# An input projection fed by unscaled x: 1/rms moved from the operand to the projected tiles

## The chip, the core and the metric

The kernel runs on one core of a Trainium2 chip. The metric is the device time of one execution in microseconds (us). The core's engines work side by side, each through its own queue: TensorE (PE in the profile, PEld for its weight loads), VectorE (DVE), ScalarE (ACT), GpSimd (POOL) and SyncE (SP, which here issues nearly all DMAs).

## What is computed

One layer of a streaming encoder, for 16 meta tokens, 64 tokens of running streams and 1024 prompt tokens at once (model width 2048):

```python
xn = _rmsnorm(h, norm_w)                       # x * rsqrt(mean(x^2) + eps) * norm_w
proj = jnp.einsum('bld,dp->blp', xn, w_in)     # 2048 -> 8208
a_b, a_c, a_x, a_z, qkv, z_b, b_logit, a_logit = jnp.split(proj, PROJ_CUTS, axis=-1)
y_a = a_b * _causal_conv(concat(state, a_c * a_x), conv_a_w) * silu(a_z)      # mixer A
qkv_c = silu(_causal_conv(concat(state, qkv), conv_qkv_w))                    # mixer B
o = gated_delta_net(l2norm(q), l2norm(k), v, beta, g)                         # in chunks
y_b = _rmsnorm(o, o_norm_w) * silu(z_b)
out = _rmsnorm(h + concat(y_a, y_b) @ w_out, final_norm_w)
```

The mean of squares is over the 2048 channels of a token; `norm_w` is one factor per channel. So the factor 1/rms of a token can be applied before the projection or after it, while `norm_w` has to be applied before it.

## The kernel before

x lies transposed (channels on the partitions) as 16 blocks of 128 channels, and its columns, the tokens, are cut into three pieces (`PIECES`): piece 0 has 336 columns (meta, streams, 256 of the prompt), pieces 1 and 2 have 384 each. Every fp32 operand is split into two exact parts, `xh`/`xl` and `wh`/`wl`, and a product is three matmuls (`xh*wh`, `xl*wh`, `xh*wl`). A *tile* of the projection is 128 output channels; per piece it takes 16 blocks x 3 = 48 matmuls into one PSUM bank of the pool `pj` (4 banks). The weights of a tile come as four chunks of 128x512 (256 KB), loaded on SP; ScalarE makes `wh` (128x512 CAST) and VectorE makes `wl` (128x512 TENSOR_TENSOR); `Weights.get` splits some chunks ahead (`ahead`), into as many places as there are buffers.

When the matmuls of a tile are done, `post` takes its pieces out of PSUM with the first stage of `a_tile`, `b_tile` or `z_tile`, and puts the rest (convolution, tanh, products) into `convs`, whose stages `pump` hands out beside the matmuls that follow, by the added-up costs `clk` of the engines; `flush_convs` hands out what is left at the end of a tile. Beside all this runs the delta net (`dn_front`, `dn_back`), whose blockwise inversion works on GpSimd (lines 787 to 796).

Before piece 0 enters the projection it is multiplied by `norm_w` alone, and its 1/rms (`rs0`) multiplies each tile as VectorE takes it out of PSUM. Pieces 1 and 2 are multiplied by 1/rms before the split: `x_later` (line 515) goes over every pair of blocks twice, first for the squares (ScalarE squares, GpSimd adds them up, line 480), then, once `x_rstd` (line 482) has the 1/rms on all partitions, to scale (GpSimd, line 534) and to split (`x_split`, line 507: ScalarE `xh`, VectorE `xl`). For piece 2 the second pass loads the pair again. The tiles of pieces 1 and 2 therefore leave PSUM without a factor: ScalarE copies them (lines 307, 338), or takes the tanh straight out of PSUM, or VectorE multiplies them by what is at hand.

`x_rstd` is a chain: 6 small matmuls sum the squares over the partitions (`ssx`), 13 VectorE instructions on 128x3 compute the inverse root, one makes diagonal matrices (`dg`), matmuls with ones spread them (`rsx`), ScalarE copies the result.

The prologue (lines 453 to 585) projects the first two channel blocks of mixer A in 24 single-piece tiles: all 8 for piece 0 (the first two side by side, chunk by chunk, with `W.ahead = 1`), then all 8 for piece 1, then all 8 for piece 2. After it come beta and decay (line 590 on) and the 56 remaining tiles, each with all three pieces, then the output projection.

VectorE executes in the order in which the code issues its instructions (the kernel is built with `manual_schedule(engines={DVE})`, line 1191). For the other engines the compiler's scheduler orders instructions by when it believes them ready; an engine then runs that order strictly.

Of the kernel before, what the change touches and what calls it, by code (L numbers as in the profile page):

```python
# [28 lines left out]
# columns of x^T: 16 meta tokens, 64 of the sample stream, 1024 of the prompt  # L29
# [5 lines left out]
# columns of the constants  # L35
# [5 lines left out]
# columns of the packed small parameters  # L41
# [4 lines left out]
class Timed:  # L46
    """An engine whose work is added up, so that the order of the program can follow it."""
# [19 lines left out]
def hymba_kernel(ctx: ExitStack, tc: tile.TileContext, hT, x_prompt, x_sample, w_in, w_ba, w_out, cst1, cst2, par,  # L67
# [27 lines left out]
    # three 128x128 blocks, their rows 416 apart and the blocks 4448, so that the twelve 32x32 blocks on the diagonals  # L95
    # are an equal step of 4448 apart too
# [30 lines left out]
    rs0 = const([P, PIECES[0][1]], "rs0")  # L127
# [8 lines left out]
    t32 = [const([P, 3, P], f"t32_{i}") for i in range(2)]  # L136
# [28 lines left out]
    # ---------------------------------------------------------------- work that goes on beside the projections  # L165
# [106 lines left out]
    def z_tile(h, p, ps):  # L272
        t = cvt("th")
        if p == 0:
            zr = cvt("zr")
            V.tensor_tensor(zr[:, :320], ps[:, 16:336], rs0[:, 16:336], ALU.mult)
            S.activation(t[:, :320], zr[:, :320], AF.Tanh, scale=0.5)
            yield
# [12 lines left out]
    def b_tile(h, w, p, ps):  # L291
        """conv, SiLU (twice its value) of a piece of q, k or v, or the gate; to the scratch memory."""
# [12 lines left out]
        else:  # L305
            n = PW
            S.copy(raw[:, 3:387], ps[:, :PW])
# [23 lines left out]
    def a_tile(j, w, p, ps):  # L331
        """the parts of mixer A of a channel tile, in the order C, X, Z, B"""
        if w == AC:
# [3 lines left out]
            else:  # L337
                S.copy(cs, ps[:, :PW])
            apc[p] = cs
        elif w == AX:  # L340
            cs = apc[p]
            u = cvt("u")
            if p == 0:
                n = 322
                t = cvt("xt", "acc")
# [7 lines left out]
            else:  # L353
                n = PW
                V.tensor_tensor(u[:, 2:386], ps[:, :PW], cs, ALU.mult)
# [7 lines left out]
        elif w == AZ:  # L363
            acc = apc[p]
            zr = cvt("za")
            if p == 0:
                V.tensor_tensor(zr[:, 0:320], ps[:, 16:336], rs0[:, 16:336], ALU.mult)
                yield
                t = cvt("th", "acc")
                S.activation(t[:, 0:320], zr[:, 0:320], AF.Tanh, scale=0.5)  # L370
                V.scalar_tensor_tensor(zr[:, 0:320], t[:, 0:320], 1.0, zr[:, 0:320], ALU.add, ALU.mult)
                V.tensor_tensor(acc[:, 0:64], zr[:, 0:64], acc[:, 0:64], ALU.mult)
                V.tensor_tensor(acc[:, 66:322], zr[:, 64:320], acc[:, 66:322], ALU.mult)
            else:
                S.activation(zr[:, :PW], ps[:, :PW], AF.Tanh, scale=0.5)
                V.scalar_tensor_tensor(zr[:, :PW], zr[:, :PW], 1.0, ps[:, :PW], ALU.add, ALU.mult)
                yield
                V.tensor_tensor(acc, zr[:, :PW], acc, ALU.mult)
        else:
            acc = apc.pop(p)  # L380
            y = cvt("ya", "raw")
            m = 320 if p == 0 else PW
            if p == 0:
                V.tensor_tensor(y[:, :m], ps[:, 16:336], rs0[:, 16:336], ALU.mult)
                yield
                V.tensor_tensor(y[:, :64], y[:, :64], acc[:, :64], ALU.mult)
# [8 lines left out]
    def post(kind, i, w, p, ps):  # L395
        """takes a piece out of PSUM at once; the rest of its work goes on beside what follows"""
# [10 lines left out]
    # ---------------------------------------------------------------- input projection  # L407
# [6 lines left out]
    jobs = [("a", j, w, (p,)) for p in ALLP for j in (0, 1) for w in AORD]  # L414
    NFIRST = len(jobs) // 3
# [10 lines left out]
    def project(js, first=lambda k: None):  # L426
        """tiles of the projection side by side: {(kind, head or block, part, piece): its place in PSUM}"""
        ps = {}
        for j in js:
            for p in j[3]:  # L430
                ps[j[:3] + (p,)] = pj.tile([P, 512], F32, tag="pj", name=f"pj{p}")
# [20 lines left out]
    # ---------------------------------------------------------------- prologue: x^T  # L452
    with ExitStack() as pro:
        xs = pro.enter_context(tc.tile_pool(name="xs", bufs=1))
        pp = pro.enter_context(tc.tile_pool(name="pp", bufs=1, space=PSUM))
        one = xs.tile([P, P], F32, tag="one", name="one")
        V.memset(one, 1.0)
        W = stream[0] = Weights(chunks[:12 * NFIRST], [P, 4, P], (wpool, "w", (2, 2)), (xs, "p", (2, 2)))

        def x_load(o, p, k, n):  # L460
            a, m = PIECES[p]
            Q.dma_start(o[:, :, :m], hT[:, k:k + n, a:a + m])

        def x_pair(p, i):
            n = PIECES[p][1]
            if p < 2:
                return raws[p][:, 2 * i:2 * i + 2, :n]
            t = xs.tile([P, 2, PW], F32, tag="xr", name="xr", bufs=3)
            x_load(t, p, 2 * i, 2)
            return t  # L470

        def x_square(t, acc, i, eng):
            n = t.shape[2]
            d = acc if i == 0 else xs.tile([P, 2, PW], F32, tag="sq", name="sq", bufs=2)
            if eng is S:
                S.activation(d[:, :, :n], t, AF.Square)
            else:
                eng.tensor_tensor(d[:, :, :n], t, t, ALU.mult)
            if i:
                G.tensor_tensor(acc[:, :, :n], acc[:, :, :n], d[:, :, :n], ALU.add)  # L480

        def x_rstd(p, acc, out):
            """(mean of the squares + eps)^-1/2 of every token, on all partitions"""
# [6 lines left out]
            yield X_LAG[2]  # L490
# [9 lines left out]
            yield X_LAG[3]  # L500
# [4 lines left out]
            S.copy(out[:, :n], ps[:, :n])  # L505

        def x_split(p, i, t):
            for j in range(2):
                k, n = 2 * i + j, t.shape[2]
                w = pk[:, K_NW + k:K_NW + k + 1]  # L510
                S.activation(xh[p][:, k, :n], t[:, j], AF.Copy, scale=w)
                V.scalar_tensor_tensor(xl[p][:, k, :n], t[:, j], w, xh[p][:, k, :n].bitcast(F32), ALU.mult,
                                       ALU.subtract)

        def x_later(p):
            acc = xs.tile([P, 2, PW], F32, tag="acc", name="sqa")
            ahead = deque()
            for i in range(NK):
                # every pair of tiles twice
                while len(ahead) < (3 if p == 2 else 1) and i + len(ahead) < NK:  # L520
                    ahead.append(x_pair(p, (i + len(ahead)) % 8))
                t = ahead.popleft()
                if i < 8:
                    x_square(t, acc, i, S)
                    yield X_LAG[0]
                    continue
                if i == 8:
                    yield X_LAG[1]
                    rsb = xs.tile([P, PW], F32, tag="rsb", name="rsb")
                    yield from x_rstd(p, acc, rsb)  # L530
                    yield X_LAG[4]
                    if p == 2:
                        x_tiles(2)
                G.tensor_tensor(t, t, rsb[:, None, :].to_broadcast([P, 2, PW]), ALU.mult)
                yield X_LAG[5]
                x_split(p, i - 8, t)
# [663 lines left out]
```

## Time and profile before

| | us |
|---|---|
| median of 3 runs | 2288.12 (2285.22 to 2289.0) |
| span of the profiled execution | 2283.8 |
| TensorE busy in it | 2211.3 (97%) |
| VectorE busy | 1335.5 (58%) |
| ScalarE busy | 640.1 (28%) |
| GpSimd busy | 940.4 (41%) |

The profiled execution has no time of its own beside its span; the span is 4.3 us under the median of the timed runs, which also hold what lies around the first and last instruction. TensorE's records overlap (one matmul begins before the one before it has left the array), so its pace is read from the distance of starts, or from counts in a window, not from the duration of one record. The granted clock is 1.00 at 2.4 GHz and 0.50 at 1.2 GHz.

### The profile page before, as it was taken

The page shows a single profiled execution, that of the slowest core. Times are in us where ns is not written, and L with a number is a line of the kernel's source. Part 1 is how long each engine was busy: PE and PEld are TensorE (multiplying, and loading weights), DVE is VectorE, ACT ScalarE, POOL GpSimd, SP SyncE. Part 2 cuts the span into 40 slices and gives each one's busy share as a digit, 9 for nine tenths or more (in the row PEclk, how much of TensorE's full clock was granted, in tenths as well). Part 3 has the DMA queues.
Part 4 walks back from the last instruction along what each step waited for, and adds up shares of the span by engine and source line. Part 5 has one row for each costly group of instructions (what it writes and reads, how often), then busy time and mean ns, then how long its engine had stood idle before and what let it go on. Part 6 is the DMA issues. An engine that isn't in the chain of part 4 may idle for free.

```text
span 2283.8 us, 36007 instructions
## 1 busy us (share of the span) xinstructions
PE 2211.3 (97%) x12938; PEld 2074.7 (91%) x12938; DVE 1335.5 (58%) x3421; ACT 640.1 (28%) x1575; POOL 940.4 (41%) x1557
## 2 busy tenths in 40 slices
PE   7799999999999999999999999999999999999998
PEld 6699889999999999999999999999999997788886
DVE  7964355667576547655664567456645345464544
ACT  5443122222222222222222222122222125444341
POOL 4520006657466645555665666655464300000000
PEclk9999999999999999999999999999999999999999
DMA  6444223232323222322222222222222238654652
GB/s 224 148 154 142 64 65 90 69 95 70 91 84 91 71 76 81 97 64 77 80 78 73 79 81 86 73 61 83 86 80 63 62 97 279 216 192 153 217 175 83
DMA packets 168790, 242.69 MB, mean 106 GB/s; under 512 B 18332, under 2 KB 92260, under 8 KB 168484
## 3 DMA queue, kind: packets, MB, share of 16 engines
q1 hardware_dynamic: 163076, 228.84, 32.1%
q0 software_dynamic: 3072, 7.11, 1.7%
q10 hardware_dynamic: 2464, 4.46, 0.5%
q8 instruction: 101, 1.65, 0.3%
q14 instruction: 77, 0.63, 0.1%
HBM read 196.14 MB, written 44.17 MB: 105 GB/s over the span
## 4 chain that ended last, share of the span: by engine, by line
PE 82%; DVE 11%; DMA 2%; issue 2%; ACT 2%; POOL 0%; SPq 0%; DVEq 0%; ACTq 0%; POOLq 0%
PE pj L83 58%; PE po L83 16%; DVE acc L61 2%; PE psy L83 2%; DVE wl L61 2%; DMA yr<-yscr 1%; PE psx L83 1%; PE psm L83 1%; PE psn L83 1%; PE pjb L83 1%; PE psu L83 1%; PE psr L83 1%; ACT jk L61 1%; DVE rot L61 1%; DVE xl L61 1%
## 5 line engine op out<-in xcount | busy, mean ns | idle before, releaser
L83 PE MATMUL pj<-xh,wh 128*128 128x384 f32 x2048 | 692.9, 338 | 8.0 <-DVE raw L61 3.5
L83 PE MATMUL pj<-xl,wh 128*128 128x384 f32 x2048 | 690.6, 337 | 1.1 <-DVE xl L61 1.1
L83 PE MATMUL pj<-xh,wl 128*128 128x384 f32 x2048 | 690.5, 337 | 0.5 <-DVE wl L61 0.4
L61 DVE TENSOR_TENSOR wl<-wr,wh 128x512 fp32r<-128x512 f32 x496 | 371.2, 753 | 343.3 <-ACT wh L61 341.7
L83 PE MATMUL pj<-x,wh 128*128 128x320 f32 (+3 forms) x2048 | 530.6, 340 | 9.4 <-ACT x L61 6.5
L61 ACT CAST wh<-wr 128x512 fp32r<-128x512 f32 x496 | 305.3, 618 | 719.1 <-PE pj L83 522.8
L792 POOL TENSOR_TENSOR tm<-eT 12x30 f32<-12x30 f32 (+4 forms) x720 | 392.1, 545 | 127.3 <-DMA eT<-e_in 72.8
L794 POOL TENSOR_TENSOR eT<-eT,tm 12x30 f32<-12x30 f32 (+4 forms) x720 | 418.5, 581 | 56.4
L83 PEld LDWEIGHTS pj<-xh,wh 128*128 128x128 f32 x2048 | 385.4, 188 | 12.7 <-issue 4.0
L83 PEld LDWEIGHTS pj<-xl,wh 128*128 128x128 f32 x2048 | 385.1, 188 | 2.1 <-DVE xl L61 1.7
L83 PEld LDWEIGHTS pj<-xh,wl 128*128 128x128 f32 x2048 | 384.9, 188 | 1.4 <-DVE wl L61 1.4
L83 PEld LDWEIGHTS pj<-x,wh 128*128 128x128 f32 x2048 | 353.7, 193 | 21.1 <-ACT x L61 6.5
L83 PE MATMUL pj<-x,wl 128*128 128x320 f32 (+3 forms) x1024 | 324.0, 316 | 11.0 <-DVE wl L61 10.9
L83 PE MATMUL po<-wh,yh 128*128 128x512 f32 x656 | 238.9, 396 | 2.6 <-DVE yh L61 1.9
L787 POOL DMA_DIRECT2D eT<-e_in x24 | 17.1, 711 | 504.6 <-DMA e_in<-bm 318.9
L83 PE MATMUL po<-wl,yh 128*128 128x512 f32 x528 | 208.9, 396 | 1.9 <-DVE wl L61 1.9
L83 PEld LDWEIGHTS pj<-x,wl 128*128 128x128 f32 x1024 | 196.9, 192 | 13.7 <-DVE wl L61 13.7
L1058 POOL TENSOR_TENSOR hres<-hres,fw 128x512 f32<-128x512 f32 x1 | 1.7, 1732 | 481.4 <-ACT hres L61 481.4
L83 PEld LDWEIGHTS po<-wh,yh 128*128 128x128 f32 x656 | 123.2, 188 | 34.0 <-ACT wh L61 3.1
L61 DVE SCALAR_TENSOR_TENSOR acc<-raw,pk,acc 128x384 f32<-128x384 f32 (+1 forms) x216 | 147.5, 683 | 5.8
L83 PE MATMUL po<-wh,yl 128*128 128x512 f32 x336 | 132.8, 395 | 0.0
L83 PEld LDWEIGHTS po<-wl,yh 128*128 128x128 f32 x528 | 99.1, 188 | 27.7 <-DVE wl L61 4.1
(254 smaller groups left out, 2191.3 us busy)
## 6 DMA issues: line engine op xcount, KB each, us to landing
wr<-in_w_in SPq DMA_DIRECT2D x320, 256.0 KB, 3.1
wr<-in_w_out SPq DMA_DIRECT2D x176, 256.0 KB, 2.7
scr<-acc SPq DMA_DIRECT2D x48, 192.0 KB, 1.9
kq<-scr SPq DMA_DIRECT2D x48, 192.0 KB, 3.0
hres<-in_x_prompt SPq DMA_DIRECT2D x32, 256.0 KB, 5.3
xr<-in_hT SPq DMA_DIRECT2D x16, 384.0 KB, 4.2
yr<-yscr SPq DMA_DIRECT2D x32, 192.0 KB, 3.4
scr<-co SPq DMA_DIRECT2D x24, 192.0 KB, 1.9
```

The lines of the kernel that those rows point to most:

```text
L61: return fn(out, *a, **k)
L83: T.matmul(out, lhsT, rhs, start=start, stop=stop)
L787: G.dma_start(eT, blocks(e_in[i]))
L792: G.tensor_tensor(t, eT[:, j + 1:32, j:j + 1].to_broadcast([12, n, j]), eT[:, j:j + 1, 0:j].to_broadcast([12, n, j]), ALU.mult)
L794: G.tensor_tensor(eT[:, j + 1:32, 0:j], eT[:, j + 1:32, 0:j], t, ALU.add)
L1058: G.tensor_tensor(o, o, fw[:r, ns], ALU.mult)
```

## The change

1. All three pieces are split unscaled (times `norm_w` only) and read once. The first pass of `x_later` is gone, as are GpSimd's additions (line 480) and multiplications (line 534). ScalarE still squares (in place, after the split); VectorE adds the squares (`x_sum`, 7 additions of two blocks per piece). Piece 2 is loaded once.
2. `rs` holds 1/rms of all three pieces, and each tile of pieces 1 and 2 is multiplied by it on VectorE as it leaves PSUM: in place of ScalarE's copy for q, k, v and C, as one more instruction for X, Z, B and the gate of mixer B. Tanh then reads SBUF.
3. The first two channel blocks go in another order and shape: block 0 for piece 0 (4 tiles, the first two side by side), block 1 for pieces 0 and 1 together (4), block 0 for pieces 1 and 2 (4), block 1 for piece 2 (4): 16 tiles and 64 chunks of weights in place of 24 and 96. They are held in PSUM (`held`, a second pool `pf` of 3 banks beside `pj`) until the 1/rms of their piece is there; `settle` then posts them in order. The splits of piece 1 are issued chunk by chunk within tile 5 (`second`), those of piece 2 within tile 9 (`third`), the sums within tiles 4, 6 and 9.
4. In `dn_back`, `tt` and `t64` share the places of `ti` and `b32`; `t32` moves to another pool. (For room in SBUF.)

The core of the diff:

```diff
     def b_tile(h, w, p, ps):
...
-            S.copy(raw[:, 3:387], ps[:, :PW])
+            V.tensor_tensor(raw[:, 3:387], ps[:, :PW], rs[p], ALU.mult)
     def a_tile(j, w, p, ps):
...
-                S.copy(cs, ps[:, :PW])
+                V.tensor_tensor(cs, ps[:, :PW], rs[p], ALU.mult)
...
-                V.tensor_tensor(u[:, 2:386], ps[:, :PW], cs, ALU.mult)
+                V.tensor_tensor(t, ps[:, :PW], rs[p], ALU.mult)
+                V.tensor_tensor(u[:, 2:386], t, cs, ALU.mult)
...
-    jobs = [("a", j, w, (p,)) for p in ALLP for j in (0, 1) for w in AORD]
-    NFIRST = len(jobs) // 3
+    jobs = [("a", j, w, ps) for j, ps in ((0, (0,)), (1, (0, 1)), (0, (1, 2)), (1, (2,))) for w in AORD]
+    NFIRST = len(jobs)
...
-                G.tensor_tensor(acc[:, :, :n], acc[:, :, :n], d[:, :, :n], ALU.add)
...
-                G.tensor_tensor(t, t, rsb[:, None, :].to_broadcast([P, 2, PW]), ALU.mult)
...
+        def x_squares(p, kc):
+            for k in range(kc, kc + 4, 2):
+                o = raws[p][:, k:k + 2, :PIECES[p][1]]
+                S.activation(o, o, AF.Square)
+
+        def x_sum(p, kc):
+            t = raws[p]
+            for o, m in (((0, 8), (2, 8)), ((4, 8), (6, 8)), ((0, 4), (2, 4)), ((0, 2),))[kc // 4]:
+                a, b = (t[:, k:k + 2, :PIECES[p][1]] for k in (o, o + m))
+                V.tensor_tensor(a, a, b, ALU.add)
...
+        def second(kc):
+            if kc not in split[1]:
+                split[1].add(kc)
+                for k in range(kc, kc + 4):
+                    x_split(1, k, raws[1][:, k, :PIECES[1][1]])
+                x_squares(1, kc)
+            settle()
+
+        def third(kc):
+            if kc not in split[2]:
+                split[2].add(kc)
+                for _ in range(2):
+                    x2_pair()
+            settle()
...
+        def settle(every=False):
+            while held:
+                _, key, ps = held[0]
+                if ("rs", key[3]) not in done:
+                    if not every:
+                        break
...
+                held.popleft()
+                if key[:3] != last[0]:
+                    flush_convs()
+                last[0] = key[:3]
+                post(*key, ps)
...
+        hooks = {2: and_settle(squares_and_load), 3: and_settle(x_sum, 0), 4: second, 5: and_settle(x_sum, 1), 8: third}
+        for i in range(2, NFIRST):
...
+            hold(1, hooks.get(i, lambda kc: settle()), pool)
+            if i in (3, 5):
+                p = i // 5
+                running[f"rs{p}"] = [0.0, known(p, x_rstd(p, raws[p]))]
```

## Rows read from the trace of the kernel before

**Rows 1.** The page: busy tenths of PE in 40 slices of 57 us.
```profile
PE   7799999999999999999999999999999999999998
```

**Rows 2.** Windows: busy us (xrecords) of PE, PEld, DVE, ACT, POOL; clock; DMA share; GB/s.
```profile
80.00:100.00 20.00, 12.62 (x64) 12.12 (x65) 19.89 (x19) 5.60 (x11) 17.15 (x9) 0.76 0.37 111
...
600.00:1000.00 400.00, 395.77 (x2511) 384.69 (x2510) 240.93 (x685) 96.12 (x278) 248.04 (x438) 1.00 0.27 80
```

**Rows 3.** Windows within the prologue, same columns.
```profile
6.50:25.00 18.50, 15.44 (x48) 12.66 (x49) 18.10 (x16) 13.16 (x25) 14.31 (x9) 1.00 0.67 233
...
43.50:50.00 6.50, 0.12 (x1) 0.01 (x1) 6.26 (x9) 2.19 (x3) 5.53 (x4) 0.66 0.18 64
...
51.20:55.70 4.50, 4.50 (x19) 4.50 (x18) 3.63 (x11) 2.54 (x4) 1.46 (x1) 0.50 0.84 260
```

**Rows 4.** Waits of PE, whole span: us in total, times, longest.
```profile
PE rsx L83 <- DVE dg L61: 13.5, 2, 7.1
PE pj L83 <- DVE wl L61: 11.3, 10, 3.3
...
PE pj L83 <- DVE raw L61: 3.5, 2, 1.9
```

**Rows 5.** Timeline of PE in the prologue: start, us, what, count, [idle before].
```profile
6.54 0.64 PE L83 MATMUL pj<-x,wh 128*128 128x322 f32 x1 [6.54 <-ACT x L61]
```
```profile
8.88 0.47 PE L83 MATMUL pj<-x,wl 128*128 128x322 f32 x1
```
```profile
32.45 0.46 PE L83 MATMUL pj<-x,wh 128*128 128x320 f32 x2
...
35.09 0.46 PE L83 MATMUL pj<-x,wh 128*128 128x320 f32 x2
```
```profile
50.02 1.54 PE L83 MATMUL rsx<-dg,one 128*128 128x128 f32 x6 [6.39 <-DVE dg L61]
```
```profile
106.62 0.33 PE L83 MATMUL pj<-xh,wh 128*128 128x384 f32 x1
```

**Rows 6.** Timeline of DVE in the prologue.
```profile
41.83 1.79 DVE L61 SCALAR_TENSOR_TENSOR rxy<-rxt,rxy 128x3 f32<-128x3 f32 x1
```
```profile
87.81 2.02 DVE L61 SCALAR_TENSOR_TENSOR cs<-u,cah,cs 128x322 f32<-128x322 f32 x1
...
102.69 0.48 DVE L61 TENSOR_TENSOR za<-pj,rs 128x320 f32<-128x320 f32 x1
...
110.83 5.38 DVE L61 SCALAR_TENSOR_TENSOR xl<-raw,pk,xh 128x384 fp32r<-128x384 f32 x10
```
```profile
128.31 0.22 DVE L61 TENSOR_SCALAR v<-ssx 128x2 f32<-128x2 f32 x2
...
129.36 0.16 DVE L61 SCALAR_TENSOR_TENSOR rxy<-rxt,rxy 128x3 f32<-128x3 f32 x1
...
131.21 0.42 DVE L61 TENSOR_SCALAR cs<-u,cah 128x384 f32<-128x384 f32 x1
...
190.70 0.69 DVE L61 TENSOR_TENSOR wl<-wr,wh 128x512 fp32r<-128x512 f32 x1 [1.42 <-ACT wh L61]
192.79 0.69 DVE L61 TENSOR_TENSOR wl<-wr,wh 128x512 fp32r<-128x512 f32 x1 [1.39 <-ACT wh L61]
...
246.83 0.56 DVE L61 TENSOR_TENSOR ya<-pj,cs 128x384 f32<-128x384 f32 x1 [5.89 <-PE pj L83]
```

**Rows 7.** Timeline of POOL and of ACT in the prologue.
```profile
102.31 2.12 POOL L480 TENSOR_TENSOR sqa<-sqa,sq 128x768 f32<-128x768 f32 x1
```
```profile
107.66 3.15 ACT L61 ACTIVATE xh<-raw,pk 128x384 fp32r<-128x384 f32 x6
```

**Rows 8.** DVE and ACT groups by form, 400 to 1800: busy, mean ns, idle before.
```profile
L61 DVE TENSOR_TENSOR raw<-pj,rs 128x256 f32<-128x256 f32 x21 | 8.8, 421 | 12.9 <-PE pj L83 12.7
...
L61 DVE TENSOR_TENSOR u<-pj,cs 128x384 f32<-128x384 f32 x10 | 5.5, 549 | 0.0
```
```profile
L61 ACT COPY raw<-pj 128x384 f32<-128x384 f32 x42 | 19.7, 479 | 61.4 <-PE pj L83 61.4
```

More of the change, by code (lines that the diff above doesn't have):

```diff
@@ L126, in hymba_kernel @@
     st_a = const([P, 8, 2, 2], "st_a")
-    rs0 = const([P, PIECES[0][1]], "rs0")
+    rs = [const([P, PIECES[p][1]], f"rs{p}") for p in range(3)]
+    rs0 = rs[0]
     gc = const([P, NH, NCH], "gc")
@@ L424, in hymba_kernel, with project @@
     stream = [None]
-    def project(js, first=lambda k: None):
+    def project(js, first=lambda k: None, pool=pj):
         ps = {}
@@ L455, in hymba_kernel, with x_rstd @@
         pp = pro.enter_context(tc.tile_pool(name="pp", bufs=1, space=PSUM))
+        pf = pro.enter_context(tc.tile_pool(name="pf", bufs=3, space=PSUM))
         one = xs.tile([P, P], F32, tag="one", name="one")
         V.memset(one, 1.0)
[L458 to L479, printed above, removed]
-                G.tensor_tensor(acc[:, :, :n], acc[:, :, :n], d[:, :, :n], ALU.add)
-        def x_rstd(p, acc, out):
+        W = stream[0] = Weights(chunks[:4 * NFIRST], [P, 4, P], (wpool, "w", (2, 2)), (xs, "p", (2, 2)))
+        def x_rstd(p, acc):
             n = PIECES[p][1]
@@ L515, in x_later @@
[L515 to L533, printed above, removed]
-                G.tensor_tensor(t, t, rsb[:, None, :].to_broadcast([P, 2, PW]), ALU.mult)
-                yield X_LAG[5]
-                x_split(p, i - 8, t)
@@ new lines, in hymba_kernel, with x2_pair, x2_rstd @@
+        x2_n, sq = [0], []
+        def x2_pair():
+            t = x2.popleft()
+            x2_n[0] += 1
+            k = 2 * x2_n[0] - 2
+            for j in range(2):
+                x_split(2, k + j, t[:, j])
+            S.activation(sqa if k == 0 else t, t, AF.Square)
+            if k:
+                sq.append(t)
+            if len(sq) > 1:
+                V.tensor_tensor(sqa, sqa, sq.pop(0), ALU.add)
+                x2_load()
+        def x2_rstd():
+            V.tensor_tensor(sqa, sqa, sq.pop(), ALU.add)
+            yield from x_rstd(2, sqa)
@@ L541, in hymba_kernel @@
+        a, n = PIECES[0]
+        for k in range(0, NK, 2):
+            if k < 4 or k % 4 == 0:
                 W.load()
-            x_load(raws[0][:, i:i + 2, :], 0, i, 2)
-        Q.dma_start(cst, cst1)
+            Q.dma_start(raws[0][:, k:k + 2, :n], hT[:, k:k + 2, a:a + n])
         V.tensor_scalar(cah, pk[:, K_CA:K_CA + 24], 0.5, None, ALU.mult)
         V.tensor_scalar(owh, pk[:, K_OW:K_OW + 1], 0.5, None, ALU.mult)
-        acc = xs.tile([P, 2, PW], F32, tag="acc", name="sqa")
-        split = set()
+        split = [set() for _ in range(3)]
@@ new lines, in hold, with known, and_settle, hook @@
+        def hold(n, first, pool):
+            js = [jobs.pop(0) for _ in range(n)]
+            held.extend((pool, key, ps) for key, ps in project(js, first, pool).items())
+        def known(p, g):
+            yield from g
+            done.add(("rs", p))
+        def and_settle(fn, *a):
+            def hook(kc):
+                fn(*a, kc)
+                settle()
+            return hook
+        def squares_and_load(kc):
+            x_squares(0, kc)
+            x1_load(8 + kc // 2)
+        hooks = {2: and_settle(squares_and_load), 3: and_settle(x_sum, 0), 4: second, 5: and_settle(x_sum, 1), 8: third}
@@ L559, in hymba_kernel @@
+        last = [None]
         W.ahead = 1
-        held = project([jobs.pop(0), jobs.pop(0)], first)
+        hold(2, first, pf)
         W.ahead = 4
-        for j in range(3, 8):
-            x_square(x_pair(0, j), acc, j, S)
-        held.update(project([jobs.pop(0)]))
-        for _ in x_rstd(0, acc, rs0):
-            pass
-        for k in range(0, NK, 4):
-            x_load(raws[1][:, k:k + 4, :], 1, k, 4)
-        running["x1"] = [0.0, x_later(1)]
-        def posts(kc):
-            if kc == 4:
-                for key, ps in held.items():
-                    post(*key, ps)
@@ L576, in hymba_kernel @@
-        for key, ps in project([jobs.pop(0)], posts).items():
-            post(*key, ps)
-        project_all(NFIRST - 4)
-        for p in (1, 2):
-            while running:
+        Q.dma_start(cst, cst1)
+        for i in range(2, NFIRST):
+            if i == 8:
+                while "rs1" in running:
+                    clk["pe"] += 0.5
+                    pump()
+                x_tiles(2)
+                sqa = xs.tile([P, 2, PW], F32, tag="acc", name="sqa")
+            while True:
+                room = [p for p, n in ((pf, 3), (pj, 4)) if sum(h[0] is p for h in held) + len(jobs[0][3]) <= n]
+                if room:
+                    break
@@ L581, in hymba_kernel @@
                 clk["pe"] += 0.5
                 pump()
-            if p == 1:
-                running["x2"] = [0.0, x_later(2)]
-            project_all(NFIRST)
-    stream[0] = Weights(chunks[12 * NFIRST:], [P, 4, P], (wpool, "w", (2, 2)))
+                settle()
+            pool = room[0]
+            hold(1, hooks.get(i, lambda kc: settle()), pool)
+            if i in (3, 5):
+                p = i // 5
+                running[f"rs{p}"] = [0.0, known(p, x_rstd(p, raws[p]))]
+            if i == 5:
+                for _ in range(4):
+                    x2_load()
@@ L590, in hymba_kernel @@
+            if i == 8:
+                running["rs2"] = [0.0, known(2, x2_rstd())]
+        settle(True)
+        flush_convs()
+    stream[0] = Weights(chunks[4 * NFIRST:], [P, 4, P], (wpool, "w", (2, 2)))
     with ExitStack() as pro:
@@ L712, in hymba_kernel @@
     EL = (5.0, 50.0)
+    t32 = [dn.tile([P, 3, P], F32, tag=f"t32_{i}", name=f"t32_{i}") for i in range(2)]
     for i in range(2):
```

101 lines of the change are left out of this document (54 added, 47 removed).

## The prediction

> **What bounds the kernel now.** I read the page first: TensorE is busy 97% of the span (table), and its only slices under nine tenths are the first two and the last [rows 1]. So TensorE sets the time, and something can be won only where it idles or runs slowly. The windows say where. Between 600 and 1000 us it idles 4 us in 400 [rows 2]; between 80 and 100 us it has 64 matmul records where 20 us would hold 136 at the pace below, while VectorE is busy 19.89 and GpSimd 17.15 [rows 2].
>
> Next, the pace. At full clock 18 piece-0 matmuls start between 32.45 and 35.09, 0.147 apart [rows 5]; for pieces 1 and 2 a chunk's 12 matmuls take 2.09 us, the distance of two `wl`, 0.175 each [rows 6]. The prologue's 24 piece-tiles thus need 8x48x0.147 + 16x48x0.175 = 56.4 + 134.4 = 190.8 us. What they got: the first matmul at 6.5, piece 1 from 106.6 [rows 5], the last result out at 246.8 [rows 6]. So piece 0 took 100.1 for 56.4 (43.7 lost) and the rest 140.2 for 134.4 (5.8 lost). Of the 43.7, the first pair took 6.5 to 32.4, 25.9 for 14.1 (11.8 lost); two `rsx` waited 13.5 for `dg`, and most of the 11.3 of waits for `wl` lie here too [rows 4]. After such a wait the granted clock is at the lower level, 1.2 GHz: 0.66 in the idle 43.5 to 50, 0.50 from 51.2 to 55.7, where 19 matmuls ran instead of 30 [rows 3].
>
> The cause is GpSimd beside VectorE. A 128x3 step of the inverse root takes 1.79 with GpSimd at work and 0.16 without; a convolution tap of 322 columns takes 2.02 [rows 6], against about 0.54 for comparable ones. The chain from `v` to `dg` takes 2.9 us undisturbed (128.31 to 131.21 [rows 6]) and kept TensorE waiting 6.7 on average when disturbed [rows 4].
>
> **The change part by part.** I number the new prologue's tiles 1 to 16 and sum what TensorE loses beyond 190.8.
>
> *Start*: 6.5, as before.
>
> *Tiles 1 and 2*. VectorE was busy 18.1 of 18.5 us here [rows 3]. Undisturbed it has 8 `wl` at 0.69 and 16 splits at about 0.5 (5.38 for ten at 384 columns) [rows 6]: 13.5 us, under TensorE's 14.1. What remains is that early matmuls run at half pace (one record takes 0.47 us at 8.88, two together 0.46 at 32.45; the granted clock says 1.00 for both, so I go by the pace) [rows 3, 5]. If half pace lasts 1 to 2 of the 4 chunk pairs (24 matmuls, 3.5 us extra each), 3.5 to 7 are lost; the bound above is today's 11.8. I take 5.
>
> *Tiles 3 and 4*: squares on ScalarE (bound by two 384-wide `xh`, 1.05 [rows 7]) and 7 sums on VectorE. No row has such a sum; between one 512-wide `wl` (0.69 [rows 6]) and two, I take 1.0 for 768 columns. Hidden behind 14 us of matmuls. Loads of piece 1 go into SP's queue ahead of weights: 0 to 3, I take 1.
>
> *Tile 5 (pieces 0 and 1)*. Here a wait replaces the removed one. VectorE obeys code order, and in each chunk it is: `wl` of the chunk three ahead, which needs the place that TensorE leaves at the previous chunk's end; then four splits; then whatever `settle` posts. So splits never run ahead of TensorE, and a chunk's first `xl` comes 0.69 + 0.54 us after the chunk starts, needed after 0.6: 0.6 to 0.7 lost in each of 4 chunks. The 2.9 us chain of piece 0 is issued in the first chunk and pushes the second's splits back by about 1. Once `rs[0]` is known, four tiles are posted at once: evacuations, three taps, tanh waits, about 5.5 us of VectorE, queued ahead of the last chunk's splits, for which TensorE then stands about 4.5. Sum 2.8 + 1 + 4.5 = 8.3; if the scheduler lets piece 0's matmuls (12 per chunk, 1.8 us) go first, 2 or less. I take 7, range 2 to 11.
>
> *Tiles 6 to 8*: 15.5 us of TensorE each; VectorE has 4 `wl` (2.8) and in tile 6 the 7 sums (7), in 7 and 8 a chain (2.9) or four posted pieces (5 to 6); nothing lost.
>
> *Tile 9 (pieces 1 and 2)*: per chunk `wl` 0.69, four splits 2.15, two sums 2.0, about 4.8 against TensorE's 4.2; ScalarE has four `xh` and two squares, 4x0.53 + 2x1.05 = 4.2 at most [rows 7], and a `wh`. Plus about 3 of posted tiles. Lost 1 to 8, taken 3.5. Tiles 10 to 16: nothing.
>
> *Matmuls of the three chains* (`ssx`, `rsx`; 1.54 at the lower clock [rows 5]): about 1.9 a piece, 5.7; present before as well. *Lower clock after stalls*: today 11 matmuls in 4.5 us, some 1.6 us, per long stall [rows 3]; I take 2, range 0 to 5.
>
> Sum: 6.5 + 190.8 + 5 + 1 + 7 + 3.5 + 5.7 + 2 = 221.5 against 246.8: **25 us gained** in the prologue, between 3 (all upper ends) and 38.
>
> *Saved beside it*: 32 chunks, each a `wl`, a `wh` and a 256 KB load, and piece 2's second load. In the prologue this is cover, not path; costed at nothing.
>
> *The steady stretch*. Pieces 1 and 2 of 56 tiles now leave PSUM on VectorE: 112 more instructions of the kind of `u<-pj`, 0.549 [rows 8], 61 us on an engine busy 241 of 400 [rows 2]; ScalarE loses copies of 0.479 [rows 8]. Who waits: a tile uses three of four banks, so the next one needs its second bank 0.45 and its third 0.97 us after the last matmul. For q, k, v the order on VectorE is piece 0's three multiplications (0.64), four small copies, piece 1's multiplication: free about 1.3 us after piece 1's last matmul, needed after 1.5. It fits by 0.2 if VectorE is not behind, and it is not: before piece 0's it idles 12.9 us in 21 cases, nearly all for TensorE [rows 8]; two waits for `raw`, 3.5 us, are all that TensorE has now [rows 4]. Z gets better, since PSUM is free after one instruction. I take +2, from -1 (the waits on ScalarE's copies go) to +10.
>
> Would GpSimd, busy 248 of 400 [rows 2], stretch these? Stretched like the tap with both operands in SBUF (2.02 [rows 6]) they would be 112 x 2.0 = 224 us of VectorE, a saturated engine. But the multiplication with one operand in PSUM at 102.69 took 0.48 [rows 6] while GpSimd's addition ran from 102.31 for 2.12 [rows 7]. So I keep 0.55. The Trainium skill, page "SBUF — State Buffer", section "Who interferes with whom", says the same by rule: VectorE with two SBUF inputs meets a GpSimd instruction that reads SBUF, with one it does not. By that rule, too, the sum stays at 61 us; the trace agrees with 0.48 against 2.02.
>
> The shared places in `dn_back` put a later write behind reads that are already ahead of it in the chain: nothing.
>
> Net -23: span 2283.8 to about 2261; the timed runs lie 4.3 above it, so **2265**.
>
> **Rivals.**
> *A. The new order in code eats it.* Tiles 5 and 9 hold TensorE at their upper ends (11 + 8), the clock falls each time (5), the first pair stays at 11.8: about 240 instead of 221.5, gain 3 to 10, 2278 to 2285, say 2280. For: code order on VectorE, the splits tied to TensorE's progress. Against: VectorE's work of the new prologue is 64 `wl` (44), 48 splits (26), 21 sums (21), three chains (9) and the 24 pieces' evacuation and taps (some 34, at 0.5 an instruction), 134 us in 220.
> *B. Slower: the evacuation.* If VectorE comes late at the end of every three-piece tile by what ScalarE used to do beside it, 56 x 0.55 = 31 us: 2288 - 25 + 31 = 2294. It decides from 0.45 us per tile end. For: slack of only 0.2 at q, k and v, and taps issued ahead. Against: the idle time before piece 0's evacuation.
> The Trainium skill, page "Perfetto Trace Analysis", section "Optimizing Scalar/DVE Operations", speaks for B: if VectorE is saturated, work should go to ScalarE, and the change does the reverse. At 60% busy the trace does not show saturation.
> *C. Nothing moves.* The prologue ends earlier but the delta net's chain, GpSimd's part of it, sets the end: 2288. Against: TensorE idles 1% from 600 to 1000 and GpSimd 38% [rows 2].
> *D. More.* The scheduler fills tiles 5 and 9 with ready matmuls: losses 2 + 1 and no clock falls, 2252.
>
> **How the numbers follow.** Forecast (2257 to 2274) 0.50, A 0.21 (a tenth of it within the bound of no change), B 0.10, C 0.06, D 0.13. A measurement can tell about 0.2%, 4.6 us. Faster: 0.50 + 0.13 + 0.19 = 0.82; the same 0.08; slower 0.10. The range leaves out B, C and the lowest tail of D: 2250 to 2284.
>
> **What would show it.** Right: no wait of `rsx` on `dg` over 2 us; 128x3 steps at 0.2; the last tile of the prologue out at 215 to 228; waits for `xl` within tiles 5 and 9, about 10 us; VectorE busy some 15 us more per 400 in the steady stretch with TensorE idling under 6 of 400. Wrong: the prologue ending after 235 (A), waits of `pj` on `raw`, `cs`, `xt` or `zr` summing over 10 us after 400 (B), or TensorE idle in new places there (C).

## The result, and the profile after

The median went from 2286.67 us (2282.09 to 2289.0, 4 runs) to 2254.62 us (2251.13 to 2256.27, 4 runs): 0.9859 of the time before, interval 0.9844 to 0.9874, some 32 us. The forecast was 2265, the gain forecast 23; rival D had given 2252. The profiled execution took 2254.53 us, its span is 2252.7, 31.1 us shorter than before.

First the page of after: busy us of each engine, and busy tenths of TensorE in 40 slices of 56 us (before: [rows 1]).

```profile
PE 2200.5 (98%) x12938; PEld 2065.4 (92%) x12938; DVE 1346.3 (60%) x3538; ACT 603.0 (27%) x1482; POOL 877.6 (39%) x1517
...
PE   8999999999999999999999999999999999999997
```

The slice that was low beside the first is full now. The place is found by cutting the span at the same three instructions in both traces. In the timeline of VectorE the last tile of the prologue leaves PSUM, in after, at:

```profile
210.50 0.56 DVE L61 TENSOR_TENSOR ya<-pj,rs 128x384 f32<-128x384 f32 x1 [5.01 <-PE pj L83]
```

It was at 246.83 before [rows 6]: **36.3 us earlier**. The tiles of beta and decay (`pjb`) and the output projection (`po`) are the next two marks (of each line: the shortest, median and longest record in ns, then the first and the last start in us):

```profile
L83 PE MATMUL pjb<-x,wbs x32: 311/317/318, 237.4 to 242.1; 128*32 128x336 f32 x32
```
```profile
L83 PE MATMUL po<-wh,yh x656: 392/395/505, 1846.7 to 2207.0; 128*128 128x512 f32 x164
```

From that last tile on, after needs 2252.7 - 210.5 = 2042.2, before 2283.8 - 246.8 = 2037.0: **5.2 us later**. The first start of `pjb` to the first start of `po` is 1609.3 here and 1605.1 before (273.1 to 1878.2), the rest to the end 406.0 and 405.6. So the gain lies in the prologue and a seventh of it is given back after it, 4.2 of the 5.2 us between `pjb` and `po`, the steady stretch. That is as forecast in kind; 36 and 5 stand where 25 and 2 were put.

The windows of after, with the columns of [rows 2]:

```profile
40.00:60.00 20.00, 19.04 (x125) 18.61 (x124) 16.79 (x47) 12.49 (x21) 0.00 (x0) 1.00 0.46 146
...
80.00:100.00 20.00, 20.00 (x128) 20.00 (x127) 12.17 (x31) 4.57 (x8) 0.00 (x0) 1.00 0.22 67
...
600.00:1000.00 400.00, 394.27 (x2478) 383.31 (x2476) 250.71 (x719) 90.02 (x256) 219.60 (x390) 1.00 0.27 78
```

Between 80 and 100 us there are 128 matmuls where before had 64, at full clock and with an idle GpSimd. In the steady stretch VectorE is busy 10 us more per 400 than in [rows 2], and TensorE idles 5.7 instead of 4.2.

### The profile page after: what moved, and what is told of

It is laid out like the page before. It is cut to its first block, busy times and chain, and to the rows that moved or that the text cites. A ratio compares the mean times of both kernels' runs of the same rounds, so it can differ in the third digit from the quotient of the medians.

```text
span 2252.7 us, 35780 instructions
## 1 busy us (share of the span) xinstructions
PE 2200.5 (98%) x12938; PEld 2065.4 (92%) x12938; DVE 1346.3 (60%) x3538; ACT 603.0 (27%) x1482; POOL 877.6 (39%) x1517
## 4 chain that ended last, share of the span: by engine, by line
PE 87%; DVE 9%; DMA 2%; ACT 1%; issue 1%; SPq 0%; DVEq 0%; ACTq 0%
PE pj L83 61%; PE po L83 17%; DVE acc L61 3%; PE psy L83 2%; PE psx L83 1%; DMA yr<-yscr 1%; PE psm L83 1%; DVE wl L61 1%; PE psn L83 1%; PE pjb L83 1%; PE psu L83 1%; PE psr L83 1%; ACT jk L61 1%; DVE rot L61 1%; PE psv L87 1%
## 5 line engine op out<-in xcount | busy, mean ns | idle before, releaser
L61 DVE TENSOR_TENSOR wl<-wr,wh 128x512 fp32r<-128x512 f32 x464 | 337.3, 729 | 334.5 <-ACT wh L61 329.7
L83 PE MATMUL pj<-x,wh 128*128 128x320 f32 (+3 forms) x2048 | 522.3, 335 | 7.0 <-ACT x L61 7.0
L61 ACT CAST wh<-wr 128x512 fp32r<-128x512 f32 x464 | 285.9, 618 | 864.0 <-PE pj L83 666.6
L847 POOL TENSOR_TENSOR tm<-eT 12x30 f32<-12x30 f32 (+4 forms) x720 | 399.8, 555 | 122.9 <-DMA eT<-e_in 68.3
L849 POOL TENSOR_TENSOR eT<-eT,tm 12x30 f32<-12x30 f32 (+4 forms) x720 | 422.9, 587 | 56.4
```

The source lines that it names most:

```text
L61: return fn(out, *a, **k)
L83: T.matmul(out, lhsT, rhs, start=start, stop=stop)
L847: G.tensor_tensor(t, eT[:, j + 1:32, j:j + 1].to_broadcast([12, n, j]), eT[:, j:j + 1, 0:j].to_broadcast([12, n, j]), ALU.mult)
L849: G.tensor_tensor(eT[:, j + 1:32, 0:j], eT[:, j + 1:32, 0:j], t, ALU.add)
```

## The experiments

Three theories stood at the start. (1) The prologue gains because GpSimd no longer disturbs VectorE. (2) It gains because x is split unscaled and once, so that no split waits for 1/rms. (3) The order of the tiles carries it. And two questions: why tiles 5 and 9 lost so little, and what the evacuation on VectorE costs. "The stretch" below is always first `pjb` to first `po`, "prologue" the start of the last `ya` that leaves PSUM before `pjb`, as above. Ratios are to the kernel before on the same chip.

### Tiles 5 and 9: TensorE in code order

```diff
-        with tc.manual_schedule(engines={mybir.EngineType.DVE}):
+        with tc.manual_schedule(engines={mybir.EngineType.DVE, mybir.EngineType.PE}):
```

> The changed kernel, with TensorE too bound to the order in which the code issues its matmuls. Theory: tiles 5 and 9 cost almost nothing in the changed kernel because the compiler's scheduler lets piece-0 (and piece-1) matmuls go ahead while VectorE splits; in code order the losses that the prediction worked out come back, about 8 us in tile 5 and 3 to 4 in tile 9, so the prologue's last result comes out at 219 to 224 instead of 210.5, with waits of pj on xl of 6 us or more. Rival: the splits were never late (VectorE had time anyway), then it stays within 210 to 213. What the delta net's matmuls lose by code order after the prologue is not the question; the span may grow by any amount there.

Measured: 2329.95 us. Most of that is the steady stretch, which the edit changes too (some 1665 us); only the prologue is compared. It ends at 228.46, 18 us later than in after and past the 219 to 224 that were expected. Timeline of TensorE, tile 5 and tile 9 (idle before in brackets):

```profile
43.45 0.44 PE L83 MATMUL pj<-xl,wh 128*128 128x384 f32 x1 [3.73 <-DVE xl L61]
...
51.53 0.45 PE L83 MATMUL pj<-xl,wh 128*128 128x384 f32 x1 [1.21 <-DVE xl L61]
...
56.90 0.45 PE L83 MATMUL pj<-xl,wh 128*128 128x384 f32 x1 [0.54 <-DVE xl L61]
...
65.19 0.69 PE L83 MATMUL pj<-xl,wh 128*128 128x384 f32 x1 [4.14 <-DVE xl L61]
...
120.50 0.45 PE L83 MATMUL pj<-xl,wh 128*128 128x384 f32 x1 [1.14 <-DVE xl L61]
126.07 0.44 PE L83 MATMUL pj<-xl,wh 128*128 128x384 f32 x1 [1.13 <-DVE xl L61]
```

Its waits in sum, whole span, against the same of after:

```profile
PE pj L83 <- DVE xl L61: 14.1, 8, 4.1
```
```profile
PE pj L83 <- DVE xl L61: 1.0, 1, 1.0
```

The sum is near the one that the prediction worked out, its parts are not. Tile 5 has one wait in each of its four chunks, 3.73, 1.21, 0.54 and 4.14, 9.6 us in sum (8.3 worked out, 7 taken), where the prediction's terms gave 0.7, 1.7, 0.7 and 5.2. The first is so long because VectorE reaches the splits, at 42.79, only behind tile 4's last sum (41.42) and a `wl`; the prediction had put the sums as hidden. The last lies behind the four tiles posted once piece 0's 1/rms is known, which VectorE works off from 58.35 to 63.9. Tile 9 has four of 1.1, 4.5 in sum (3.5 taken). The waits for `xl` are 13.1 us more than in after; with them go 1.6 before piece 2's `ssx` and a mean granted clock of 0.91 in the windows from 40 to 60 and from 60 to 80. In after, where the compiler's scheduler orders TensorE, the waits for `xl` are gone but one; its timeline of TensorE:

```profile
40.22 0.34 PE L83 MATMUL pj<-xh,wh 128*128 128x384 f32 x1
40.39 0.46 PE L83 MATMUL pj<-x,wh 128*128 128x322 f32 x2
...
42.62 1.23 PE L83 MATMUL ssx<-one,raw 128*128 128x1 f32 x12
...
44.84 0.33 PE L83 MATMUL pj<-xl,wh 128*128 128x384 f32 x1
...
54.25 0.44 PE L83 MATMUL pj<-xl,wh 128*128 128x384 f32 x1 [0.96 <-DVE xl L61]
```

After one matmul of piece 1, piece 0's (`x`, 322 columns) and the chain's `ssx` (the six matmuls of the code are 12 records) run until 44.84, and the first with `xl` starts only then, when VectorE is past its first splits. One wait of 0.96 is left. So rival D's mechanism is shown: ready matmuls fill the tiles with two pieces.

### GpSimd's part, from both sides

Back into the changed kernel, the sums of squares alone:

```diff
-                V.tensor_tensor(a, a, b, ALU.add)
+                G.tensor_tensor(a, a, b, ALU.add)
```

(and the same for piece 2's additions, lines 528 and 532).

> The changed kernel, with its 21 additions of squares on GpSimd instead of VectorE (one part of the change undone). Theory (GpSimd's reads of SBUF hold up VectorE): VectorE loses 21 x 0.9 us of work, but wl, splits and the 128x3 steps beside the 21 additions of about 2 us are stretched; the chains come later by what the last additions take. The prologue ends 3 to 15 us later, at 214 to 225, and the time is 2257 to 2269. Rival (contention is of little account, the order of tiles and fewer chunks make the gain): the prologue ends within 1 us of 210.5, or earlier.

Measured: 2280.58 us, 0.9969 [0.9959, 0.9980]; prologue 233.12, 22.6 later than after and past what was expected. Timelines of POOL, TensorE and VectorE:

```profile
21.78 14.31 POOL L504 TENSOR_TENSOR raw<-raw 128x672 f32<-128x672 f32 x7 [21.33 <-ACT raw L61]
```
```profile
36.15 2.40 PE L83 MATMUL ssx<-one,raw 128*128 128x1 f32 x12 [7.48 <-POOL raw L504]
```
```profile
78.95 0.48 DVE L61 TENSOR_TENSOR cs<-pj,rs 128x322 f32<-128x322 f32 x1
79.35 6.43 DVE L61 TENSOR_TENSOR wl<-wr,wh 128x512 fp32r<-128x512 f32 x3
```

Two costs are seen. GpSimd needs 2.04 us a sum, and TensorE stands 7.5 us before `ssx` (10.0 before all three). And beside the sums, which run from 76.2 to 87.5, VectorE's work with two operands in SBUF stretches: three `wl` in 6.43, 2.1 each against 0.69 [rows 6], while the multiplication out of PSUM just before them takes 0.48. TensorE's waits for `xl` are 6.8 us against 1.0, and its mean granted clock is 0.83 from 20 to 40 and from 140 to 160. What each cost comes to of the whole was not separated. 21 additions give back 22.6 of the 36.3 us that the prologue had won.

Out of the kernel before, GpSimd's work of the prologue alone (to VectorE, three of piece 0's squares to ScalarE):

```diff
-                G.tensor_tensor(acc[:, :, :n], acc[:, :, :n], d[:, :, :n], ALU.add)
+                V.tensor_tensor(acc[:, :, :n], acc[:, :, :n], d[:, :, :n], ALU.add)
...
-                G.tensor_tensor(t, t, rsb[:, None, :].to_broadcast([P, 2, PW]), ALU.mult)
+                V.tensor_tensor(t, t, rsb[:, None, :].to_broadcast([P, 2, PW]), ALU.mult)
...
-                    x_square(x_pair(0, i), acc, i, G)
+                    x_square(x_pair(0, i), acc, i, S)
```

> The kernel before, with the prologue's additions and multiplications on VectorE instead of GpSimd (16 multiplications and 21 additions of about 0.95 us each, some 35 us more for VectorE) and the first squares on ScalarE; order of tiles, second pass and 96 chunks stay. Theory: of the 36 us that the prologue gained, most comes from taking GpSimd away from beside VectorE: the waits of rsx on dg fall from 13.5 to under 4 us, no stretch of half clock is left after them, and the last result comes out at 222 to 234 instead of 246.8; time 2264 to 2276. Rival (the order of tiles, one read and fewer chunks make the gain): it stays at 240 or later.

Measured: 2270.44 us, 0.9922 [0.9900, 0.9944]; prologue 233.37, 13.4 earlier than before. Its waits for `dg` and for `xh`, then its window of the first tile of piece 1, then VectorE, ScalarE and TensorE at the start of it:

```profile
PE rsx L83 <- DVE dg L61: 0.3, 1, 0.3
```
```profile
PE pj L83 <- ACT xh L61: 5.7, 5, 2.5
```
```profile
80.00:100.00 20.00, 14.82 (x39) 9.57 (x39) 13.61 (x21) 8.60 (x16) 0.00 (x0) 0.64 0.01 3
```
```profile
77.87 0.95 DVE L61 TENSOR_TENSOR raw<-raw,rsb 128x768 f32<-128x768 f32 x1
...
78.86 1.12 ACT L61 ACTIVATE xh<-raw,pk 128x384 fp32r<-128x384 f32 x2 [1.31 <-DVE raw L61]
79.50 1.15 DVE L61 SCALAR_TENSOR_TENSOR xl<-raw,pk,xh 128x384 fp32r<-128x384 f32 x2 [0.68 <-ACT xh L61]
...
79.52 0.44 PE L83 MATMUL pj<-xh,wh 128*128 128x384 f32 x1 [2.49 <-ACT xh L61]
```

The wait for `dg` is gone with GpSimd (13.5 us before [rows 4]), so theory 1 holds for it. Divided as the prediction divides the kernel before, piece 0 takes 72.6 us here (6.9 to 79.5) for 56.4 of matmuls: 16.2 are lost in place of 43.7. The rest loses 233.4 - 79.5 - 134.4 = 19.5, where before lost 5.8. There a new stall shows: 20 us have only 39 matmuls at a mean granted clock of 0.64, since scaling, `xh` and `xl` go pair by pair once 1/rms is known, and TensorE waits for them.

Before has a stall at 80 to 100 us too [rows 2], but another one: there TensorE is still in piece 0, waiting for `dg` and `wl`, up to 106.6. Its `rsx` for piece 1 ran at 83.54 (here at 76.20, behind piece 0's last matmul), so GpSimd scaled all of piece 1 beside the rest of piece 0, and TensorE hardly waited for the splits; the timeline of POOL and the waits of TensorE in before:

```profile
85.75 16.61 POOL L534 TENSOR_TENSOR raw<-raw,rsb 128x768 f32<-128x768 f32 x8 [2.77 <-ACT rsb L61]
```
```profile
PE pj L83 <- DVE xl L61: 1.1, 2, 0.7
```

So taking GpSimd away saves 27.5 us over piece 0, and 13.7 are lost again where piece 1 waits for its 1/rms and its feed, which before the rest of piece 0 covered. That is what theory 2 can win, seen from here. GpSimd's own 2 us a sum and its effect on VectorE are not separated by this run.

### Unscaled, without GpSimd, but in the old order

```diff
-    jobs = [("a", j, w, ps) for j, ps in ((0, (0,)), (1, (0, 1)), (0, (1, 2)), (1, (2,))) for w in AORD]
+    jobs = [("a", j, w, (p,)) for p in ALLP for j in (0, 1) for w in AORD]
```

(with the splits and sums moved to tiles 9, 10 and 17, since pieces 1 and 2 begin in 9 and 17; with 24 tiles there are 96 chunks of weights again).

> The changed kernel, with its first two channel blocks piece by piece again (24 tiles of one piece, 96 chunks; the splits of piece 1 in tile 9, of piece 2 in tile 17). Theory: the tiles of two pieces are needed because they double TensorE's matmuls per chunk while VectorE splits the next piece. With one piece, a chunk is 2.1 us of TensorE against 0.69 + 2.15 us of VectorE in tile 9, and against 4.8 in tile 17 with the sums, and nothing that is ready can go ahead: 4 and 11 us lost by VectorE alone, and more by half clock after many short waits; the prologue ends 12 to 25 us later, at 222 to 236. Rival (only the missing GpSimd work and the single pass matter): under 215.

Measured: 2267.32 us, 0.9911 [0.9898, 0.9925]; prologue 218.15, 7.6 later than after, between what the theory (222 to 236) and its rival (under 215) gave. Windows of it at the change to piece 2, and its waits:

```profile
140.00:160.00 20.00, 16.79 (x88) 14.74 (x88) 15.12 (x26) 11.18 (x18) 0.00 (x0) 1.00 0.55 159
```
```profile
PE pj L83 <- DVE xl L61: 3.4, 2, 1.7
```

Where a piece starts alone, nothing ready can go ahead of its splits, and 88 matmuls stand in 20 us that hold 117 in after. The three theories now have sizes, in the order in which these kernels add them: 246.8 to 233.4 with GpSimd off (13.4), to 218.2 with x unscaled and read once (15.2), to 210.5 with the new order and its 64 chunks, which were not separated (7.6). The shares depend on that order: GpSimd's 13.4 are what is left of 27.5, and put back last, its sums alone cost 22.6.

### Reading piece 2 twice

```diff
+            if i in (9, 10):
+                for k in range(8 * (i - 9), 8 * (i - 8), 2):
+                    t = xs.tile([P, 2, PW], F32, tag="xr", name="xr", bufs=4)
+                    Q.dma_start(t, hT[:, k:k + 2, PIECES[2][0]:PIECES[2][0] + PW])
```

> The changed kernel, with piece 2 of x loaded a second time (8 loads of 384 KB into places that nothing reads), behind tiles 10 and 11. Theory, as the prediction had it: the second read was cover and not path; the prologue ends within 1 us of 210.5, the time stays within 2252 to 2257. Rival: the loads hold up weights in SP's queue (1.3 us each at the prologue's DMA rates), 3 to 10 us.

Measured: 2253.73 us (2250.4 to 2257.21); prologue 211.15. The second load, behind tiles 10 and 11 into places that nothing reads, costs nothing that can be measured, which is what the prediction put for it.

### The price of the evacuation

The 56 later tiles take pieces 1 and 2 out of PSUM as before; this leaves out their 1/rms. The core of it:

```diff
-            V.tensor_tensor(raw[:, 3:387], ps[:, :PW], rs[p], ALU.mult)
+            S.copy(raw[:, 3:387], ps[:, :PW])
```

> The changed kernel, with pieces 1 and 2 of the 56 later tiles leaving PSUM as in the kernel before (ScalarE copies, tanh out of PSUM, products without a factor); it leaves out their factor 1/rms. Theory: the stretch from the beta matmuls to the first matmul of the output projection, 1605.1 before and 1609.3 after, goes back to 1604 to 1606, since the waits of pj on cs, xt, raw and zr (11.6 us, 7.5 before) are what it grew by; time 2249 to 2252. Rival: the 4 us are the delta net's chance alignment; then the stretch moves by under 1.5 us or the other way.

Measured: 2253.29 us (2250.05 to 2255.52), the stretch 1605.4 against 1609.3 in after. The stretch is shorter, as expected, but the time hardly moved, since in the profiled execution the prologue ended at 214.48, 4 us later, though no instruction of it was edited. Timeline of TensorE there:

```profile
43.07 1.77 PE L83 MATMUL ssx<-one,raw 128*128 128x1 f32 x12 [1.29 <-DVE raw L61]
...
48.01 0.52 PE L83 MATMUL pj<-xh,wl 128*128 128x384 f32 x1
```

And of ScalarE, at the weights of tile 4:

```profile
34.48 0.62 ACT L61 CAST wh<-wr 128x512 fp32r<-128x512 f32 x1 [2.07 <-DMA wr<-in_w_in]
```

A wait of 1.29 before the small `ssx` matmuls, then half pace until 50.5; the window 40 to 60 has 96 matmuls at a clock of 0.83, after's has 125 at 1.00. A weight split of tile 4, and with it the sums, came 0.9 us later than in after: its `wh` waited 2.07 us for the load of the weights and began at 34.48, in after 1.13 us, until 33.55. Why the load landed later stays open.

Then the other division of the work: ScalarE copies q, k, v and C out of PSUM, VectorE multiplies in SBUF one stage later.

```diff
-            V.tensor_tensor(raw[:, 3:387], ps[:, :PW], rs[p], ALU.mult)
+            S.copy(raw[:, 3:387], ps[:, :PW])
+            yield
+            V.tensor_tensor(raw[:, 3:387], raw[:, 3:387], rs[p], ALU.mult)
```

> The changed kernel, with q, k, v and C of pieces 1 and 2 copied out of PSUM by ScalarE, as before, and multiplied by 1/rms on VectorE in the next stage, out of and into SBUF (VectorE has the same number of instructions). Theory: the 4 us that the steady stretch lost are TensorE's waits for a PSUM bank at the end of a tile, not VectorE's load; the stretch from the beta matmuls to the output projection falls from 1609.3 to 1605 to 1607, and the waits of pj on raw and cs from 7.5 to under 5. Rival (VectorE's load itself): it stays at 1609 or grows, since the multiplications now have both operands in SBUF beside GpSimd.

Measured: 2265.74 us, 0.9905 [0.9891, 0.9918]; prologue 211.87, the stretch 1623.5, 14 us longer than in after. Waits of TensorE that changed much, whole span, here and then in after:

```profile
PE pot L87 <- DVE on L61: 8.7, 5, 3.4
PE psq L87 <- DMA kq<-scr: 4.5, 2, 3.5
PE pj L83 <- ACT raw L61: 2.9, 2, 2.5
PE psr L83 <- DVE sn L61: 2.6, 3, 1.1
PE psx L83 <- DVE b L61: 2.2, 2, 1.7
```
```profile
PE pj L83 <- DVE raw L61: 4.2, 4, 1.9
PE pj L83 <- DVE cs L61: 3.3, 2, 2.3
PE pj L83 <- DVE xt L61: 2.9, 3, 1.5
PE pj L83 <- DVE zr L61: 1.2, 2, 0.7
PE pot L87 <- DVE on L61: 1.0, 2, 0.7
```

The theory that freeing PSUM on ScalarE saves time failed. The waits for VectorE's `raw` and `cs` go (0.2 in all is left, and 2.9 for ScalarE's `raw`), and larger ones come in the delta net: for operands that VectorE makes there (`on`, `sn`, `b`; the last two 0.3 each in after) and for the load of `kq` (0.9 in after), whose source mixer B writes. The rival had named this outcome, 1609 or more, with VectorE's load as its cause; but VectorE is busy 876.7 us from 400 to 1800, and 876.9 in after. Why it is late was not separated: its multiplication is longer, and it stands one stage later in its queue. The multiplication takes longer from SBUF as well (groups by form, 400 to 1800, here and then in after, 300 to 1850):

```profile
L61 DVE TENSOR_TENSOR raw<-raw,rs 128x384 f32<-128x384 f32 x40 | 26.8, 670 | 0.0
```
```profile
L61 DVE TENSOR_TENSOR raw<-pj,rs 128x384 f32<-128x384 f32 x44 | 24.1, 548 | 0.0
```

Taken over the kernels, without the two whose stretch was changed otherwise (TensorE in code order and this one), the stretch is 1603.5 to 1605.4 where pieces 1 and 2 leave PSUM as before (before, 1605.1; GpSimd off, 1603.5; the old evacuation, 1605.4) and 1609.3 to 1614.5 where VectorE multiplies them (after, 1609.3; the sums on GpSimd, 1611.1; second read, 1612.0; later chain, 1611.7; piece by piece, 1614.5). Each is one execution, and executions of after alone have spans from 2249.1 to 2254.5; but the two groups do not overlap. The price is 4 to 11 us, on average 1611.7 - 1604.7 = 7.

### Starting the chains of 1/rms later in the code

```diff
-                running[f"rs{p}"] = [0.0, known(p, x_rstd(p, raws[p]))]
+                running[f"rs{p}"] = [max(clk.values()) + 3.0, known(p, x_rstd(p, raws[p]))]
```

> The changed kernel, with the chains of pieces 0 and 1 started 3 us later in the code's own clock. In the run with the old evacuation, whose prologue has the same code, TensorE stood 1.29 us before ssx, for the last sum of piece 0, then ran about 6 us at the lower clock, and the prologue ended at 214.5 instead of 210.5. Theory: whether that happens depends on when the weights of tile 4 arrive, and it is what spreads the runs of the changed kernel (2251.1 to 2256.3); with ssx later there is no wait, the prologue ends at 210 to 211.5, and the runs lie within 2 us, around 2252. Rival: the spread is something else; it stays at 4 to 5 us.

Measured: 2260.63 us (2256.32 to 2266.07); prologue 213.72. The wait before `ssx` is 0.2 here (1.29 in the run above with the old evacuation, none in after), but `rsx` waited for `dg`:

```profile
PE rsx L83 <- DVE dg L61: 2.6, 2, 2.3
```

Worse by 3 us in the prologue, and the runs lie 10 us apart. The theory fell; why runs of the changed kernel differ by 5 us among themselves stays open.

## Why the prediction was right, and where it was off

The time, 2254.6, lies nearest to rival D. Tiles 5 and 9 ran as D had it, to which the prediction gave 0.13; the terms named there (2, 1 and no clock falls in place of 7, 3.5 and 2) give 2265 - 9.5 = 2255.5, not the 2252 that was written. In the same way "all upper ends", with 11.8 for the first pair, add up to a gain of 5, not 3.

*What bounds the kernel*: right. TensorE sets the time, and the 43.7 us lost over piece 0 were what could be won; the whole prologue of after loses 210.5 - 6.4 - 190.8 = 13.3.

*The cause*: right for the kernel before, not the whole of the gain. GpSimd beside VectorE was named as the cause; with GpSimd off, piece 0 loses 16.2 of the 43.7. But the prologue as a whole wins only 13.4 of the 36.3 by that, since feeding piece 1 after its 1/rms, which costs before only 1.1 us of waits, then becomes the stall. The prediction did not ask what the slow piece 0 covered. The sum was not touched by this, since it built the new prologue up from its own steps and did not subtract causes.

*Tiles 1 and 2*: right, to the tenth of a us by luck, since 5 was a choice between 3.5 and 7. The timeline of TensorE in after shows the first pair at half pace until about 15.4 and done at 25.66; forecast were 6.5 + 14.1 + 5 = 25.6.

```profile
14.59 0.74 PE L83 MATMUL pj<-x,wh 128*128 128x322 f32 x2
15.39 0.46 PE L83 MATMUL pj<-x,wh 128*128 128x322 f32 x2
...
25.66 0.45 PE L83 MATMUL pj<-x,wh 128*128 128x320 f32 x2
```

*Tiles 3 and 4*: 39.77 - 25.66 = 14.1, nothing lost where 1 was taken. A sum of 672 columns cost 0.85, one of 768 columns 0.95 (1.0 taken), from the timeline of VectorE, with the first splits of piece 1 behind one:

```profile
41.49 0.85 DVE L61 TENSOR_TENSOR raw<-raw 128x672 f32<-128x672 f32 x1
...
42.86 2.20 DVE L61 SCALAR_TENSOR_TENSOR xl<-raw,pk,xh 128x384 fp32r<-128x384 f32 x4
```

*Tiles 5 and 9, and the clock after them*: **the step that failed**. 7 + 3.5 + 2 were taken; after shows one wait of 0.96 for `xl`, and the granted clock is 1.00 in every window of 20 us from 20 to 220. From 39.77 to the end, 170.7 us hold 162.6 of matmuls and about 5.1 of chain matmuls; some 3 are lost, 12.5 were taken. The prediction argued with VectorE's code order and took TensorE to wait where the code puts the next matmul. It had written down that the scheduler orders TensorE by readiness, and priced that at "2 or less", but kept it for rival D at 0.13. The run with TensorE in code order has waits of 14.1 for the 10.5 that the prediction gave tiles 5 and 9, so the mechanism was there and sized roughly, but for an order that TensorE does not run. The term at nothing in tiles 3 and 4, the sums, was among those waits: 3.73 us of them lie behind the last sum.

*Chains*: right. `ssx` and `rsx` take about 1.7 a piece (1.9 taken), and `rsx` waits 0.3 for `dg` where "not over 2" was forecast.

*The steady stretch*: right in sign and mechanism, low in size. The instruction costs 548 ns on average (549 taken), with GpSimd busy 219.6 of 400 us beside it. But TensorE's waits on the evacuation rose from 7.5 us (`raw`, ScalarE's `raw`, and smaller ones) to 11.6, and the stretch by 4 to 11 against 2 taken and 10 as upper end: this term was sized too low. The slack of 0.2 at q, k and v does not always hold: VectorE comes late by up to 2.3 us (`cs`), in 11 places, not at the end of each of 56 tiles, as rival B needed. The mark given for B, over 10 us of such waits, was passed by 1.6, so it was set too low to tell B apart.

The Trainium skill, page "SBUF — State Buffer", section "Who interferes with whom", had given no stretch for an instruction with one operand in SBUF; 548 ns agrees with it. Its other half, two operands in SBUF beside a GpSimd that reads SBUF, shows in the 2.1 us of a `wl` beside GpSimd's sums.

*The other marks*: `rsx` on `dg` (0.3), the 128x3 steps (0.16 to 0.22) and TensorE's idle time in the stretch (5.7 of 400) came as forecast. The last tile came out at 210.5, before the 215 to 228 that were given; waits for `xl` were 1.0 in place of about 10; and VectorE is busy 10 us more per 400 in place of 15, for which the reason was not looked for.

*The difference in all*: 2265 - 2254.6 = 10.4 is 11.0 too little gained in the prologue, less 3.2 too little lost after it, 2.4 from what lies around the span, and rounding. For the last, 4.3 was taken as the median of three runs less the span of another execution; each timed run of before whose span is known is 2.2 to 2.4 above it, of after 1.8 to 2.0.

## What to carry to other kernels

A factor that belongs to the output can be taken out of the operand's path: then the operand's splits need not wait for it, and tiles whose factor is late can be held in PSUM. Side by side in one tile, a piece that is ready and one that is just being split let the scheduler cover the late operand, so before pricing a wait on TensorE ask in which order TensorE itself will run, not the engine that feeds it. GpSimd's cheap-looking additions cost twice, by their own 2 us and by what they do to VectorE; and here one multiplication by VectorE straight out of PSUM cost less than a copy by ScalarE and the multiplication in SBUF. And a stall that is taken away can bring out another that it had covered.

## What the runs showed of the hardware that was not expected

The granted clock did not fall with each wait. After the 0.96 us at 54.25 in after it stayed at 1.00, the 2.4 GHz level. With the old evacuation a wait of 1.29 followed by one-column `ssx` matmuls (1.77 us) brought 6 us at the other level: 0.50 granted from 44.8 to 50.5. At the same place a wait of 1.17 (piece by piece) did not, and neither did one of 2.34 before `rsx` (later chain); the 20 us windows around both show 1.00:

```profile
42.02 1.34 PE L83 MATMUL ssx<-one,raw 128*128 128x1 f32 x12 [1.17 <-DVE raw L61]
```
```profile
58.40 0.87 PE L83 MATMUL rsx<-dg,one 128*128 128x128 f32 x6 [2.34 <-DVE dg L61]
```

Where TensorE waited 0.2 to 1.1 us again and again, the mean was 0.64 over 20 us (before with GpSimd off, 80 to 100). In the first 9 us of matmuls the column shows 1.00 while three start per 0.81 us in after, later three per 0.44; before has the same slow start [rows 3, 5]. What holds that pace was not tried.

A GpSimd addition of 128x672 took 2.04 us, where VectorE needs 0.85 for the same.
